# A transformer block on one core: squares of branch and output weights moved to other units, some merge and norm steps reordered, one tail chunk's weights asked for later

## The chip, the cores and the metric

The kernel runs on one core of a Trainium2 chip. The metric is device time in microseconds (us) of one execution. A core has a matrix engine (PE in the profile, with its weight load PEld), three elementwise engines (VectorE, DVE; ScalarE, ACT; GpSimd, POOL) and SyncE (SP), whose queue issues nearly all DMAs here. Each engine works through its own instructions in the order in which the program lists them, and waits at an instruction whose inputs or buffers are not ready. So what a step costs depends on its place in its engine's list.

## What is computed

One layer on 2048 tokens of width 1024, in float32:

```
h    = rms_norm(x) * gain
proj = h @ w_in          # q,k,v of branch A; q,k,v of branch B in 3 groups; gates ga, gb; merge logits mg
ya   = banded attention A (8 query heads, 2 key heads, window 128, sink logit), per-head norm of q and k
yb   = three dilated attentions (dilation 1, 4, 16; 8 heads each), combined by softmax denominators
br_a = (ya * silu(ga)) @ w_branch_a ;  br_b = (yb * silu(gb)) @ w_branch_b
g    = sigmoid(mg + b_merge)
out  = x + (g[0]*br_a + g[1]*br_b) @ w_out
```

## The kernel before

**Number format.** Every float32 operand of a matmul is split into two float16 parts, high and low, and a product is three float16 matmuls (high-high, low-high, high-low). Weights are first scaled by a power of two. For that scale the sum of squares of the weights is needed: ACT squares a piece with a running sum per partition (`w_square`, `g_square`, `piece_square`), a small PE matmul against ones adds the partitions (`norm_sum`, line 219), and six small DVE steps make the power of two (`norm_pow`, line 222 on). For the branch weights a and b and the output weights, one scale each comes from eight *pieces* (`piece_load` line 1160, `piece_square` 1165, two halves of 128x1024 each; `piece_sum` and `piece_pow` at the end). A piece is only squared: the weights themselves are loaded again in the tail.

**Stages.** A start (about 70 us) norms and transposes x into XH and XL. Then come 14 *units* of 8 *pairs* each, 112 pairs: unit 0 and 2 are branch A (4 query heads, one key head), the others branch B (2 heads of one dilation group). A pair projects two blocks of 128 tokens (48 matmuls of 128x384, line 735), norms and splits q and k, transposes them by DMA (`kq`), and computes attention items of earlier pairs: logits (line 905), `maxima` (line 920, with the bias added), exps, a split, a transpose by DMA (`pt`), and the product with the values (line 954). Some pairs also carry a *fill*: 24 matmuls of 128x512 for a gate chunk (line 359). Units 4, 7, 10 and 13 are dilation group 0, in which the three groups are merged for each quarter (`b_merge_q`): `collect` (POOL, line 1118), `exponents` (DVE), exps (ACT), `factors` (DVE), `products` (POOL), `sums` (DVE); since an item runs nearly five pairs behind its projection, half of a unit's merges fall into the next unit, 5, 8 or 11 (or behind the last pair). A merged half goes to a `YPart`: `halves` (ACT, line 1034), `turn_halves` (a DMA transpose on SP, line 1038, `ya<-yh`), `join` (ACT, line 1043), `gate` and `top` (DVE), `store`. The tail (from about 1366 us) makes the merge gates, the branch products and the output product in a form with seven instead of eight block products, for which sums of blocks of x are made during the units (`x_sums`).

**The order of the work.** It is written out by hand. Every step is given a time in units of one pair (in the tail, in us); a heap sorts the steps by time, and they are put into the program between the matmuls in this order. The times do no more than set the order on each engine and each DMA queue. `NORM` holds the times, from the end of a pair, of: square, stats, newton, scale, gain, hi, lo, swap, turn (steps of q and k). `B_MERGE` holds collect, exponents, exps, factors, products, sums; `A_MERGE` those of branch A, whose fourth value is the time of the first product. `Y_DMA` holds load, halves, turn_halves, join, gate, top, store. A B item's steps stand at `LAGS['B']` from a time of 0.387 or 0.887 in a pair, its `out` at 0.223 or 0.723 two pairs on, and its `z_store` (a DMA issued by ACT, line 993) 0.1 behind.

**Raw weights.** One tile of 128x8x384 (`wraw`, one buffer) takes in turn the next unit's weights (`w_load`, from 0.4 in a unit) and, from 5.9 on, a *window*: the gate chunk in its first third, if the unit prepares one (units 2, 4, 7, 10, 13 and two early ones), and a piece in the other two thirds. `N_PREP` holds, in a unit, the time of the first of four piece loads of 256 KB (`B_GAP[2]` = 0.231 apart) and of the two piece squares. In the tail `T_P` holds for each chunk n the times of its weights' preparation (`prep`: load at +0.3, gains from +5.5, squares from +8.5, sum at +15.6, power at +16.1, split from +17.0) and of its T blocks (`w_sums`).

```
    for k in range(8):
        u = 3 + k
        ...
        for j in range(4):
            at(t + N_PREP[0] + B_GAP[2] * j, piece_load, u, k, j)
        for half in range(2):
            at(t + N_PREP[1 + half], piece_square, u, k, half)
    chain([(98.0, piece_sum), (98.3, piece_pow)])
```

Of the kernel before, what the change touches and what calls it, by code (L numbers as in the profile page):

```python
# [63 lines left out]
NPAIR = 8 * NU  # L64

EVAC = (0.015, 0.025, 0.099)
NORM = (0.028, 0.136, 0.32, 0.626, 0.744, 0.904, 0.962, 1.033, 1.118)
LS = 2.887
LAGS = {'A': (-0.21, 0.002, 0.019, 0.144, 0.276, 0.337, 0.417), 'B': (-0.156, -0.001, 0.042, 0.169, 0.19, 0.379, 0.525)}
LV = {'A': 1.111, 'B': 1.829}  # L70
OUT = 0.007
B_LAST = 0.763
DRAIN = 0.8
A_MERGE = (0.085, 0.258, 0.51, 0.671, 1.503, 0.761)
B_MERGE = (-0.037, 0.133, 0.333, 0.507, 0.665, 1.053)
Y_PART = (-0.097, 0.483, 0.709, 0.893, 0.943)
Y_DMA = (-0.097, 0.45, 0.55, 1.05, 1.13, 1.2, 1.25)
Y_MAX_DMA = (0.026, 1.4, 1.45)
GATE = (-0.123, -0.064, 0.329)
W_STEP = (0.4, 0.465, 1.9, 0.445, 4.197, 0.146, 0.342)  # L80
W_MAX = (3.762, 3.892)
G_PREP = (5.907, 6.882, 7.102, 7.671, 7.712, 7.812, 7.942)
N_PREP = (6.3, 7.15, 7.753)
B_GAP = (0.4, 0.138, 0.231)
Y_FREE = 0.15
G_LATE = {6: 0.2, 9: 0.2, 7: 0.2}
Y_MAX = (0.026, 0.815, 0.839)
Y_MAX_A = (0.026, 1.9, 1.95)
X_LOAD = (15.23, 15.24, 18.98, 18.99, 23.61, 30.1, 23.62, 30.09, 30.58, 30.56, 30.55, 30.57, 33.96, 32.57, 32.55, 34.01)
X_SQ = (18.89, 18.9, 18.99, 19, 24.3, 30.11, 24.51, 30.24, 30.89, 30.62, 30.62, 30.62, 37.13, 44.55, 39.37, 40.39)  # L90
X_GROUPS = {(0,): (19.24, 19.72, False), (1,): (19.75, 19.76, False), (2, 3): (19.9, 20.54, False), (4, 5, 6, 7): (30.37, 30.48, False), (8, 9, 10, 11): (30.9, 33.71, False), (12, 13, 14, 15): (44.56, 44.57, False)}
# [9 lines left out]
X_END = (68.1, 71.1, 75.1)  # L101
X_TH = 1.2
X_SC = (0.25, 0.25, 0.25, 0.0625)
X_SUM = ((3, 14.5), (19, 33), (48, 60.5), (71.5, 84.5), (97, 108)), 0.35, 109.0
T_Y = (2.0, 0.8, 1.6, 1.5, 4.0, 26.0, 0.5, 1.3, 2.1, 1.6, 2.0)
T_P = ((0, 0.0, 0.03), (1, 7.0, 31.0), (2, 37.5, 60.5), (3, 69.4, 92.4), (4, 105.8, 128.8), (5, 142.2, 165.2))
T_O = ((2, 38.0, 48.0), (3, 68.0, 80.0), (0, 104.0, 116.0), (1, 140.0, 152.0))
T_OB = ((2, 40.0), (3, 50.0))
T_G = (173.0, 183.0, 193.0, 194.5)
# [21 lines left out]
def block_kernel(tc, x, w_units, w_gate, w_mrg, w_brn, w_out, w_bra, gain, qkg, sink, bias_a, bias_b, b_merge, out):  # L131
# [329 lines left out]
    def chain(steps):  # L461

        steps = sorted(steps, key=lambda e: e[0])
        done = [0]

        def go(k):
            if done[0] < k or steps[k][1](*steps[k][2:]) is False:
                at(now[0] + .04, go, k)
            else:
                done[0] = k + 1  # L470

        for k, e in enumerate(steps):
            at(e[0], go, k)
# [245 lines left out]
    class Pair:  # L719
# [19 lines left out]
        def plan(self, e):  # L739
# [4 lines left out]
            steps = (self.square, self.stats, self.newton, self.scale, self.gain, self.hi, self.lo, self.swap, self.turn)  # L744
            for d, f in zip(NORM, steps):
                at(e[1] + d, f)
# [327 lines left out]
    def a_merge(t, un, za, q):  # L1074
# [21 lines left out]
        def product(c):  # L1096
            y = wk.tile([128, 4, 2, HD], F32, name="ya")
            hs = slice(2 * c, 2 * c + 2)
            G.tensor_tensor(y[:], za[:, :, hs, 0:HD], e1[:, :, hs].unsqueeze(3).to_broadcast([128, 4, 2, HD]), OP.mult)
            YPart(2 * j + c, q, y[:].rearrange("p b h e -> p b (h e)")).plan(t + A_MERGE[3 + c] + A_MERGE[5])  # L1100

        for d, f in zip(A_MERGE, (exponents, exps, factors)):
            at(t + d, f)
        for c in range(2):
            at(t + A_MERGE[3 + c], product, c)

    def b_merge_q(t, un, zz, q):
# [31 lines left out]
        def sums():  # L1139
# [5 lines left out]
            if q % 2:  # L1145
                YPart(4 + j, q // 2, un.y).plan(t + B_MERGE[5] * (B_LAST if t > NPAIR + 1 else 1))

        for d, f in zip(B_MERGE, (collect, exponents, exps, factors, products, sums)):
            at(t + d * (B_LAST if t > NPAIR + 1 else 1), f)
# [58 lines left out]
        chain([(t + G_PREP[1] + .1 * i, g_gain, c, i) for i in range(2)]  # L1208
              + [(t + d, f, c) for d, f in zip(G_PREP[2:6] + (G_PREP[6] + G_LATE.get(c, 0),), (g_square, g_sum, g_pow, g_hi, g_lo))])
    for k in range(8):  # L1210
        u = 3 + k
        t = 8 * u
        if all(w != u for _, w, _ in FILLS):
            at(t + G_PREP[0] - .01, window, u)
        for j in range(4):
            at(t + N_PREP[0] + B_GAP[2] * j, piece_load, u, k, j)
        for half in range(2):
            at(t + N_PREP[1 + half], piece_square, u, k, half)
    chain([(98.0, piece_sum), (98.3, piece_pow)])
    for q in range(4):  # L1220
        fill.setdefault(NPAIR + q, []).extend((mg_step, q, k) for k in range(2))

# [42 lines left out]

    at(X_SUM[2], xs_early)
    times = spread(128, X_SUM[0])
    for k in range(8):
# [4 lines left out]
    while t < NPAIR or heap or any(k >= t for k in fill):  # L1273
        u, j = divmod(t, 8)
# [645 lines left out]
```

## Time and profile before

| | |
|---|---|
| time, median of 3 executions | 1900.66 us (1900.16 to 1904.5) |
| profiled execution | 1902.51 us, of which 1900.7 us span of the core |
| start | 0 to 70 us |
| 14 units | 70 to 1295 us |
| last items, merges and fills | 1295 to 1366 us |
| tail | 1366 to 1901 us |
| B pair without a fill, unit 5 | 9.3 us |
| A pair, unit 2 | 12.5 us without a fill, 17.8 with one |

The profile is of one execution. An engine is *busy* while it works on an instruction, not while it waits. For PE the ends are modelled, and a new matmul starts while the one before is still in the pipeline; therefore a stand of PE shorter than that overlap does not show as idle. The list of waits says for each engine and line what ended the idle time before it, with the total, the number of times and the longest. The table by stage gives the busy time of each engine in a stretch of the span; the stretch less PE's busy time is PE's idle time there. A timeline gives, for one engine, start, length, line, operation, out<-in and, in brackets, the idle time before it and what ended it; `SPq` and `ACTq` are DMA issues of these engines. The granted clock is 1.00 throughout.

### The profile page before, as it was taken

What the parts mean: (1) busy time and instruction counts of PE and PEld (TensorE: products, weight loads), DVE (VectorE), ACT (ScalarE), POOL (GpSimd) and SP (SyncE); (2) the same over time, 40 slices, a digit from 0 to 9 for tenths busy, and PEclk for the clock granted to TensorE, in tenths of its full rate; (3) what the DMA queues carried; (4) which work ended last, traced back from release to release, by engine and by line L of the source; (5) the groups of instructions that cost most, each with busy time, mean ns of one, the idle gap of its engine ahead of it and who ended that gap; (6) DMA issues with size and microseconds to landing.
All of it is one profiled execution on the core that took longest, in us unless ns stands there. A gap on an engine that the chain in (4) does not pass through costs nothing.

```text
span 1900.7 us, 39497 instructions
## 1 busy us (share of the span) xinstructions
PE 1882.0 (99%) x13493; PEld 1182.4 (62%) x13493; DVE 1379.7 (73%) x3691; ACT 1157.6 (61%) x2692; POOL 762.6 (40%) x1782
## 2 busy tenths in 40 slices
PE   8999999999999999999999999999999999999999
PEld 6556666677766687666876668865444444444444
DVE  7579886898887777878778787878457565767412
ACT  8468776787776776777767776666345553422100
POOL 2233343334455554555555654455110001222543
PEclk9999999999999999999999999999999999999999
DMA  8559988798978787798877978678455445988763
GB/s 290 126 98 181 219 166 164 151 184 182 203 145 185 151 174 162 151 183 152 176 153 145 196 139 167 123 180 184 149 196 172 143 146 189 294 252 256 252 245 145
DMA packets 643929, 340.68 MB, mean 179 GB/s; under 512 B 493840, under 2 KB 577424, under 8 KB 642320
## 3 DMA queue, kind: packets, MB, share of 16 engines
q1 hardware_dynamic: 625296, 329.51, 73.2%
q10 hardware_dynamic: 18432, 8.66, 1.9%
q8 instruction: 105, 1.72, 0.4%
q14 instruction: 96, 0.79, 0.1%
HBM read 141.97 MB, written 77.33 MB: 115 GB/s over the span
## 4 chain that ended last, share of the span: by engine, by line
PE 74%; DVE 9%; DMA 6%; ACT 4%; issue 3%; POOL 3%; SPq 1%; DVEq 0%; ACTq 0%; POOLq 0%
PE pj L735 38%; PE pj L359 11%; PE fps L359 6%; PE s L905 5%; PE fps L1787 5%; PE pv L954 4%; PE fps L1575 2%; PE pj L1787 2%; DMA wraw<-in_w_mrg_dram 1%; PE pj L1575 1%; DMA kq<-spl 1%; PE pj L635 1%; DVE wl L279 1%; DMA mtd<-mm 1%; DVE pr L920 1%
## 5 line engine op out<-in xcount | busy, mean ns | idle before, releaser
L735 PE MATMUL pj<-wh,XH 128*128 128x384 f16 x1792 | 584.6, 326 | 4.0 <-DVE vt L767 3.3
L735 PE MATMUL pj<-wh,XL 128*128 128x384 f16 x1792 | 586.2, 327 | 0.0
L735 PE MATMUL pj<-wl,XH 128*128 128x384 f16 x1792 | 584.8, 326 | 0.0
L735 PEld LDWEIGHTS <-XH 128*128 128x128 f16 x3584 | 411.2, 116 | 154.3 <-issue 5.7
L735 PEld LDWEIGHTS <-XL 128*128 128x128 f16 x1792 | 207.6, 116 | 67.4
L920 DVE CUSTOM_DVE_ANT_0 pr<-s,b,ubuf 128x256 f32<-128x256 f32 (+3 forms) x512 | 218.4, 463 | 36.9 <-PE s L905 36.0
L937 DVE SCALAR_TENSOR_TENSOR p<-pr,p 128x512 f16<-128x512 f32 (+2 forms) x256 | 190.4, 744 | 17.8 <-ACT p L933 16.1
L812 POOL COPY spl<-spl 128x256 f16<-128x256 f16 (+1 forms) x224 | 89.5, 428 | 229.7 <-DVE spl L807 227.3
L933 ACT ACTIVATE p<-pr 128x512 f16<-128x512 f32 (+2 forms) x256 | 159.0, 621 | 6.1 <-DMA pt<-p 0.2
L905 PE MATMUL s<-kq 128*128 128x256 f16 (+3 forms) x1168 | 147.9, 254 | 2.0 <-DMA kq<-spl 1.8
L752 ACT ACTIVATE rw<-pj 128x256 f32<-128x256 f32 (+1 forms) x224 | 86.1, 385 | 103.4 <-PE pj L735 95.2
L954 PEld LDWEIGHTS <-pt 128*128 128x128 f16 x3024 | 125.4, 97 | 35.3 <-DMA pt<-p 1.5
L797 POOL TENSOR_TENSOR rw<-rw,g 128x256 f32<-128x256 f32 (+1 forms) x112 | 92.4, 825 | 122.9 <-DVE rw L791 82.3
L954 PE MATMUL pv<-vt,pt 128*128 128x65 f16 (+1 forms) x3024 | 132.7, 193 | 1.1 <-DMA pt<-p 1.1
L905 PEld LDWEIGHTS <-kq 128*128 128x128 f16 x1184 | 101.5, 98 | 43.6 <-DMA kq<-spl 3.5
L310 POOL TENSOR_TENSOR rs_t<-rs_y 128x8 f32<-128x8 f32 (+1 forms) x112 | 44.4, 396 | 208.9 <-DVE rs_y L302 174.3
L791 DVE TENSOR_TENSOR rw<-rw,qr 128x512 f32<-128x512 f32 (+1 forms) x112 | 86.8, 775 | 54.0 <-POOL qr L319 53.6
L1728 POOL TENSOR_TENSOR kp<-kp,fg 128x512 f32<-128x512 f32 x32 | 45.4, 1421 | 190.6 <-DVE fg L1721 190.6
L1787 PEld LDWEIGHTS <-M 128*128 128x128 f16 x684 | 66.9, 98 | 78.8 <-issue 0.6
L359 PE MATMUL fps<-Y,wh 128*128 128x512 f16 x384 | 114.2, 379 | 0.0
L928 ACT ACTIVATE pr<-pr,z 128x128 f32<-128x128 f32 (+2 forms) x256 | 98.7, 438 | 24.3 <-DVE z L920 24.1
L1787 PE MATMUL fps<-wt,M 128*128 128x512 f16 (+1 forms) x516 | 110.3, 374 | 0.3 <-DVE pr L1802 0.3
(289 smaller groups left out, 3838.4 us busy)
## 6 DMA issues: line engine op xcount, KB each, us to landing
wraw<-in_w_units_dram SPq DMA_DIRECT2D x56, 384.0 KB, 4.5
mtd<-mm SPq DMA_DIRECT2D x56, 256.0 KB, 3.9
M<-mtd SPq DMA_DIRECT2D x8, 1792.0 KB, 9.7
zd<-z ACTq DMA_DIRECT2D x128, 66.0 KB, 2.6
zz<-zd SPq DMA_DIRECT2D x64, 132.0 KB, 2.8
xt<-in_x_dram SPq DMA_DIRECT2D x16, 512.0 KB, 9.4
gtd<-yo SPq DMA_DIRECT2D x32, 256.0 KB, 3.0
xsd<-sx SPq DMA_DIRECT2D x32, 256.0 KB, 3.1
```

Source lines behind the costliest of these rows:

```text
L359: out.append(lambda w=w, xx=xx, ch=ch, i=i: T.matmul(ps[:], lhsT=w[:, ch, c0:c0 + 128], rhs=xx[:, ch, ts], start=(i == 0), stop=(i == n - 1)))
L735: out.append(lambda lhs=lhs, rhs=rhs, ch=ch, k=k: T.matmul(ps[:, :384], lhsT=lhs[:, ch, :], rhs=rhs[:, ch, :], start=(k == 0), stop=(k == ...
L791: V.tensor_tensor(q, q, self.rr[:, :n].unsqueeze(2).to_broadcast([128, n, HD]), OP.mult)
L797: G.tensor_tensor(k, k, GT[un.br][:].unsqueeze(1).unsqueeze(1).to_broadcast([128, 2, un.nk, HD]), OP.mult)
L812: G.tensor_copy(sp[:, i, nh:, :, :], sp[:, i, nq:nh, ::-1, :])
L905: T.matmul(self.sv[j][:, o:o + k1 - k0], lhsT=q[:, h, qo:qo + 128], rhs=kt[:, un.nq + kh + v * un.nk, k0:k1], start=(v == 0), stop=(v == 1))
L920: V.tensor_tensor_reduce(out=self.pv[:, j, self.p0:self.p0 + W], in0=self.sv[j], in1=un.bias[:, self.h0 + j, self.b0:self.b0 + W], scale=I ...
L928: A.activation(v, v, AF.Exp, bias=self.stat(j), scale=-1.0)
L933: A.activation(self.sp[:, :128 * n], self.pr, AF.Copy, scale=PSC)
L937: V.scalar_tensor_tensor(self.sp[:, 128 * n:], self.pr, PSC, self.sp[:, :128 * n], OP.mult, OP.subtract)
L954: T.matmul(self.po[:, j, :w], lhsT=p[:, n * j + s, :], rhs=un.v[key][:, vh, c0:c0 + w], start=(k == 0 and s == 0), stop=(k == 2 and s == n ...
L1787: mm.append(lambda ch=ch, k=k, w=w, i=i: T.matmul(ps[:, :cols.stop - cols.start], lhsT=m[:, a, ch, k, :], rhs=wt[w][:, b, ch, cols], start ...
```

## The change

Nothing is added to or taken from the computation, and no tile changes. Times are changed, so steps change places:

- The eight pieces are loaded and squared in units 2, 3, 4, 6, 7, 9, 10 and 12 (`PIECE_U`) instead of 3 to 10; units 5 and 8 have none. Their loads start at 6.473 instead of 6.3 in the unit; the squares keep their times, 7.15 and 7.753. `piece_sum` moves from 98 to 107.
- In `NORM`, stats moves from 0.136 to 0.172 and hi from 0.904 to 0.841.
- In `B_MERGE`, collect moves from -0.037 to 0.034 and exponents from 0.133 to 0.278; in `A_MERGE`, the first product from 0.671 to 0.753.
- In `Y_DMA`, turn_halves moves from 0.55 to 0.576 and join from 1.05 to 1.042; two times of `Y_MAX_A` move by 0.003 and 0.018.
- In `X_SUM`, the fourth stretch for the sums of x starts at 71.842 instead of 71.5, which spreads all 128 steps a little differently, and the early loads of the sums for the tail go from 109 to 111.19.
- In `T_P`, the preparation of tail chunk 1 starts at 10.0 instead of 7.0 us.

```diff
-NORM = (0.028, 0.136, 0.32, 0.626, 0.744, 0.904, 0.962, 1.033, 1.118)
+NORM = (0.028, 0.172, 0.32, 0.626, 0.744, 0.841, 0.962, 1.033, 1.118)
...
-A_MERGE = (0.085, 0.258, 0.51, 0.671, 1.503, 0.761)
-B_MERGE = (-0.037, 0.133, 0.333, 0.507, 0.665, 1.053)
+A_MERGE = (0.085, 0.258, 0.51, 0.753, 1.503, 0.761)
+B_MERGE = (0.034, 0.278, 0.333, 0.507, 0.665, 1.053)
 Y_PART = (-0.097, 0.483, 0.709, 0.893, 0.943)
-Y_DMA = (-0.097, 0.45, 0.55, 1.05, 1.13, 1.2, 1.25)
+Y_DMA = (-0.097, 0.45, 0.576, 1.042, 1.13, 1.2, 1.25)
...
-N_PREP = (6.3, 7.15, 7.753)
+N_PREP = (6.473, 7.15, 7.753)
 B_GAP = (0.4, 0.138, 0.231)
+PIECE_U = (2, 3, 4, 6, 7, 9, 10, 12)
+PIECE_SUM = 107.0
...
-Y_MAX_A = (0.026, 1.9, 1.95)
+Y_MAX_A = (0.023, 1.882, 1.95)
...
-X_SUM = ((3, 14.5), (19, 33), (48, 60.5), (71.5, 84.5), (97, 108)), 0.35, 109.0
+X_SUM = (((3, 14.5), (19, 33), (48, 60.5), (71.842, 84.5), (97, 108)), 0.35, 111.19)
...
-T_P = ((0, 0.0, 0.03), (1, 7.0, 31.0), (2, 37.5, 60.5), (3, 69.4, 92.4), (4, 105.8, 128.8), (5, 142.2, 165.2))
+T_P = ((0, 0.0, 0.03), (1, 10.0, 31.0), (2, 37.5, 60.5), (3, 69.4, 92.4), (4, 105.8, 128.8), (5, 142.2, 165.2))
...
     for k in range(8):
-        u = 3 + k
+        u = PIECE_U[k]
         t = 8 * u
...
-    chain([(98.0, piece_sum), (98.3, piece_pow)])
+    chain([(PIECE_SUM, piece_sum), (PIECE_SUM + 0.3, piece_pow)])
```

## The prediction, made before the changed kernel ran

> **What bounds the kernel now.** I read the page's busy table first, then who TensorE (PE) waits for, then the busy time by stage, and last the engines in order of time around the few stages where PE stands still.
>
> ```profile
> span 1900.7 us, 39497 instructions
> ...
> PE 1882.0 (99%) x13493; PEld 1182.4 (62%) x13493; DVE 1379.7 (73%) x3691; ACT 1157.6 (61%) x2692; POOL 762.6 (40%) x1782
> ```
>
> PE is busy for 1882.0 of 1900.7 us. The change removes no matmul. So nothing in it can bring more than the 18.7 us in which PE stands still, and a step that is taken off another engine is worth only what ends a PE wait sooner. The waits of PE say what ends them (in all, times, longest):
>
> ```profile
> PE pj L735 <- DVE vt L767: 3.3, 5, 0.8
> PE fps L219 <- ACT wl L247: 2.2, 2, 1.8
> PE s L905 <- DMA kq<-spl: 1.8, 1, 1.8
> PE pv L954 <- DMA pt<-p: 1.1, 1, 1.1
> ```
>
> The table by stage tells where. Columns: length, then busy time of PE, weight load, VectorE (DVE), ScalarE (ACT), GpSimd (POOL), then granted clock, DMA share and GB/s.
>
> ```profile
> 0.00:75.00 75.00, 68.68 (x439) 44.12 (x440) 56.52 (x161) 57.02 (x111) 18.97 (x20) 1.00 0.74 228
> 75.00:490.00 415.00, 413.04 (x3655) 282.58 (x3654) 344.82 (x905) 304.28 (x693) 154.88 (x417) 1.00 0.83 167
> 656.50:668.20 11.70, 9.63 (x82) 6.79 (x81) 7.27 (x22) 8.70 (x20) 4.33 (x14) 1.00 1.22 201
> 812.60:899.70 87.10, 86.25 (x667) 57.80 (x666) 67.83 (x211) 61.44 (x148) 50.51 (x123) 1.00 0.85 167
> 899.70:928.00 28.30, 28.17 (x243) 23.29 (x242) 21.31 (x69) 19.59 (x49) 12.69 (x41) 1.00 0.93 189
> 1053.70:1140.50 86.80, 86.20 (x667) 57.72 (x666) 69.52 (x215) 60.37 (x147) 50.67 (x123) 1.00 0.83 162
> 1140.50:1150.80 10.30, 9.51 (x82) 6.93 (x81) 5.82 (x20) 6.43 (x15) 3.30 (x13) 1.00 0.68 142
> 1150.80:1366.00 215.20, 214.83 (x1655) 146.18 (x1654) 162.62 (x504) 130.79 (x343) 104.15 (x271) 1.00 0.70 155
> 1366.00:1395.00 29.00, 27.19 (x128) 12.25 (x127) 10.71 (x22) 12.01 (x22) 4.03 (x4) 1.00 0.93 299
> ```
>
> The start, which the change leaves alone, holds 6.32 us of the idle time. Units 0 to 3 (75 to 490) hold 1.96; the last pair of unit 5 (656.5 to 668.2) 2.07; the last pair of unit 11 (1140.5 to 1150.8) 0.79; units 8 and 11 before their last pairs 0.85 and 0.60; unit 8's last pair with the two behind it 0.13; everything from unit 12 to the tail 0.37; the first 29 us of the tail 1.81. These nine stretches, less the start, make 8.58 us: that is about all the change can win.
>
> **The pieces leave units 5 and 8.** Units 5, 8 and 11 follow the units that merge branch B, carry the second half of that merge, and have the same fills. Only unit 11 has no pieces. So it is the model of what 5 and 8 become. In all three ACT stands at `join` (L1043) for the transposed `ya`, the key split `hi` (L803) is behind it, and PE soon runs out:
>
> ```profile
> 657.13 1.36 ACT L1043 ACTIVATE yh<-ya 128x1024 uint16<-128x1024 uint16 x1 [2.34 <-DMA ya<-yh]
> ...
> 1138.84 0.33 ACTq L993 DMA_DIRECT2D zd<-z  x1
> 1141.64 1.37 ACT L1043 ACTIVATE yh<-ya 128x1024 uint16<-128x1024 uint16 x1 [2.83 <-DMA ya<-yh]
> 1142.87 0.60 ACT L803 ACTIVATE spl<-rw 128x512 f16<-128x512 f32 x1
> ```
>
> ACT waits as long without pieces (2.83 us in unit 11) as with them (2.34 in unit 5), so the pieces do not cause that wait. What they add in unit 5 is behind it: the key transposes then go out among the piece loads at a DMA share of 1.22, against 0.68 in unit 11. So unit 5 should go from 2.07 to unit 11's 0.79: -1.28. Unit 8 pays nothing today at that place with its pieces; between 0 and +0.79 I take +0.2. The pair behind unit 8 can give back at most 0.13: -0.1.
>
> **`join` and `hi` in ScalarE's order.** In a B pair (1.0 of planner time) one item stands at 0.887, so its `z_store` (line 993) is planned at 0.823 and `join` at 0.826. With 1.042, `join` moves to 0.818, ahead of `z_store`; `hi` moves from 0.904 to 0.841 and stays behind both. So where ACT stands at `join`, the 0.33 us of `z_store`'s issue, which today passes before that wait (1138.84), now falls between it and `hi`, and evacuation and PSUM release (L752, L761, L767) come 0.33 later. Units 5, 8 and 11 each have one such place: +0.33 in 5 and 11, and in 8 it is inside the +0.2. The zd written there is read two units later; nobody waits.
>
> In the pair after a unit's first, `hi` at 0.841 now goes ahead of the first two weight squares (0.9):
>
> ```profile
> L244 ACT ACTIVATE wl<-wraw,gn x112: 598/605/624, 47.5 to 1183.7; 128x384 f16<-128x384 f32 x112
> ```
>
> So keys are ready up to 1.2 us sooner once per unit and the squares 0.6 later. PE waits in none of these places, so I take 0; the squares are needed by `w_sum` 1.9 pairs on.
>
> **The merge steps.** `collect` (0.686 to 0.757) goes behind `gain` on POOL; `exponents` (0.856 to 1.001) goes behind `maxima` and the key's `lo` on DVE.
>
> ```profile
> 1054.75 0.19 POOL L1118 COPY zz<-nmB 128x4 f32<-128x4 f32 x1
> ...
> 1057.15 0.18 DVE L1122 TENSOR_TENSOR bm_e<-bm_n,zz 128x12 f32<-128x12 f32 x1
> 1057.25 0.47 DVE L920 CUSTOM_DVE_ANT_0 pr<-s,b,ubuf 128x256 f32<-128x256 f32 x1
> ...
> 1058.66 0.28 DVE L767 SCALAR_TENSOR_TENSOR vt<-pj,vt 128x128 f16<-128x128 f32 x1
> ```
>
> `maxima` thus starts about 0.3 us earlier (two small instructions) and `gain` 0.2 earlier. But both stay ahead of `v_lo` (L767), which is what PE waits for in the first pairs of units 8 and 11: the same work stands before it, so the 0.85 and 0.60 us stay. The merge's exps at 1.056 on ACT, queued behind the item's exps, now waits for `exponents` up to some tenths, with the item's `hi` behind it; `maxima`'s 0.3 pays that back. Sum 0. `stats` at 0.172 goes behind the gate weights' `lo` in units 5, 8 and 11 and behind one `maxima` in A units; a delay of about 1.3 us (1059.91 below) which the scale step 0.45 pair later covers.
>
> ```profile
> 1059.91 1.28 DVE L412 SCALAR_TENSOR_TENSOR gl<-wraw,ubuf,gh 128x1024 f16<-128x1024 f32 x1
> ```
>
> **The pieces come to units 2 and 12.** Unit 12 has room: 0.37 us of PE idle in the 215 us around it. Unit 2 is an A unit whose window also loads gate weights, and it is full:
>
> ```profile
> 366.80:379.30 12.50, 12.50 (x144) 8.57 (x141) 11.46 (x31) 10.63 (x23) 3.86 (x11) 1.00 1.02 207
> 379.30:391.90 12.60, 12.60 (x155) 9.09 (x152) 12.18 (x33) 11.12 (x23) 7.15 (x14) 1.00 0.94 168
> 391.90:409.80 17.90, 17.90 (x171) 13.22 (x168) 17.16 (x47) 15.95 (x34) 6.38 (x19) 1.00 0.91 164
> ```
>
> The next fence has the length of a B pair (its first figure), the squares, their only wait, and the landing of half of the piece loads:
>
> ```profile
> 647.20:656.50 9.30, 9.30 (x82) 6.88 (x81) 6.87 (x20) 6.25 (x15) 3.77 (x13) 1.00 0.93 189
> ...
> L1167 ACT ACTIVATE wraw<-wraw x16: 1039/1046/1069, 493.9 to 1052.9; 128x1024 f32<-128x1024 f32 x16
> L1167 ACT ACTIVATION_READ_ACCUMULATOR wraw<-wraw x16: 180/187/198, 494.8 to 1053.9; 128x1 f32 x16
> ...
>   DMA wraw<-in_w_out_dram: 0.9, 1
> ...
> DMA to landing us min/median/max: 2.9/4.1/6.3
> ```
>
> Two squares of 1.05 + 0.19 make 2.5 us on top of ACT's 11.12 in a 12.6 us pair: 13.6, so ACT falls 1 us behind and makes it up in the next pair (15.95 of 17.9). The projections alternate between two PSUM banks, so an evacuation has half a pair in hand, and the cost lies between 0 and 2.5; I take +0.4.
>
> **Piece loads later everywhere.** Loads start at 6.473 instead of 6.3, so all four pass behind the next item's `pt` transpose (0.412) or the later one (0.912) on SP's queue. The first square still comes at 7.15, so its second load has 0.446 instead of 0.619 pair: in a pair of 9.3 us (the row above) 4.1 instead of 5.8 us. Against the landing row (2.9/4.1/6.3) ACT now waits 0 at the median and 2.2 at worst, in each of eight units. Behind it stand an `out` and the evacuation, which waits for PE anyway:
>
> ```profile
> ACT rw L752 <- PE pj L735: 95.2, 92, 3.3
> ```
>
> 95.2 us over the 92 evacuations that wait is 1.0 us of cover each, and I take 0. By the Trainium skill ("DMA: Bandwidth & Descriptors", Anatomy of one DMA, given for GpSimd's path) a transfer costs about 2.0 us plus bytes over 436 GB/s; for 256 KB I estimate 2.6 us, by which no square would ever wait and the slower case below would drop out. The median of 4.1 here, beside other transfers, speaks against relying on that.
>
> **The tail chunk.** `T_P` moves chunk 1's load, gains, squares, sum and power all 3.0 us later.
>
> ```profile
> 1376.50 4.60 SPq L195 DMA_DIRECT2D wraw<-in_w_mrg_dram  x4
> 1381.20 1.82 SPq L1581 DMA_DIRECT2D mgd<-fd  x2
> ...
> 1389.83 0.63 ACT L247 ACTIVATE wl<-wraw 128x512 f16<-128x512 f32 x1 [0.28 <-POOL wraw L200]
> ...
> 1390.60 0.17 PE fps L219
> ```
>
> Today PE comes to the sum matmul (L219), waits 1.8 us for the last square, and goes on at 1390.60, so it came at 1388.8. Three us later in PE's order is 1391.8. The load was held until 1376.5 by the queue ahead, not by its plan (7.3 us after 1366), so at 10.3 it starts almost as before, only behind one `fd` store: 0.91 us. The squares end near 1391.5, before PE comes: -1.8. Were the load really 3 us later, the gain would be 0. The chunk's T blocks are due at 31.0 as before; they end about a microsecond later, some 2 us ahead of their matmuls.
>
> **The rest.** The T-sums of x move by at most 0.34 pair, A merges by 0.08; both act where PE idles 1.96 us in all (75 to 490), so a gain is at most that, a loss of that size is possible, taken 0. `piece_sum` (three powers, some 18 small DVE steps) moves to unit 13's third pair with as much room as today's; `xs_early`'s tiles are read only in the tail, over four pairs later. Both 0.
>
> **Sum.** -1.28 + 0.33 (unit 5) + 0.2 (unit 8) - 0.1 (behind it) + 0.33 (unit 11) + 0.4 (unit 2) - 1.8 (tail) = -1.9 us. The profiled execution took 1902.51 (span 1900.7 and 1.8 around it), 1.85 above the median of 1900.66. So 1900.6 for such an execution and **1898.8** as the median. About 0.3%, 5.7 us, is what a measurement tells from no change.
>
> **The rivals.** (1) *More waits go than I count.* Keys split ahead of the squares, transposes ahead of piece loads, `maxima` ahead of `exponents` and shifted x sums also end the 8.58 us. All of it: 1892.1; three quarters: 1894.2. For it: nearly all these waits end in a transpose or in DVE's order. Against: none of the moved steps passes `v_lo`. (2) *The tail gain does not arrive* since the load slips the full 3 us behind SP's stores, and unit 5 keeps its wait: without the 1.8 and the 1.28 the sum is +1.2, 1901.8. The load's 1376.5 start speaks against it. (3) *Slower: ACT waits for piece loads.* At the worst landing the first square waits 2.2 us in eight units; past the 1.0 us of cover 1.2 x 8 = 9.6 goes to PE: 1908.4. It decides once loads land over about 5.1 us (4.1 + 1.0) after issue, on busy queues such as units 2, 3 and 4. For it: loads go out behind transposes, DMA share near 1. Against: a square waited only once, 0.9 us, in the trace of before, and pieces fit today in units as full.
>
> **How the numbers follow.** Forecast 0.56 (its own range 1896.5 to 1901.5), rival 1 0.18, rival 2 0.12, rival 3 0.14. Faster by over 0.3% is rival 1: 0.18; slower is rival 3: 0.14; the others are within: 0.68. The range 1893.0 to 1904.5 takes in most of rival 1 and all of rival 2, with the runs' spread (1900.16 to 1904.5); outside stay rival 3 and the end of rival 1, 0.2.
>
> **What would show it.** Right: no PE wait at L219 near 1390, PE idle under 1.2 us at the end of unit 5, about 1.1 at the end of unit 11, `join` directly followed by `zd<-z`, units 2 and 12 with PE idle under 0.5. Wrong: L1167 among ACT's long waits for DMA, a new PE wait in units 2 and 3, or idle gone from 75 to 490 and from the first pairs of 8 and 11.

## The result, and the profile after

The changed kernel takes 1912.08 us (median of four executions, 1910.44 to 1914.06) against 1900.88 for the kernel before in the same session (1900.16 to 1904.5): a ratio of 1.0056, 95% interval 1.0038 to 1.0073. That is slower by 11.2 us, outside the predicted range, on the side of rival 3 and 3.7 us beyond its price. In the kernels from here on every line number is 2 higher than before (L735 is now L737, `hi` L805, the piece loads L1165, their squares L1169).

The profile's page and its list of waits (in all, times, longest), changed kernel:

```profile
span 1911.6 us, 39478 instructions
...
PE 1885.1 (99%) x13493; PEld 1182.6 (62%) x13493; DVE 1384.0 (72%) x3691; ACT 1154.6 (60%) x2692; POOL 769.6 (40%) x1782
```

```profile
PE pj L737 <- DVE vt L769: 6.3, 8, 1.3
PE fps L221 <- ACT wl L249: 2.6, 1, 2.6
PE s L907 <- DMA kq<-spl: 2.1, 2, 1.4
PE pt L221 <- DVE wm L228: 1.5, 1, 1.5
```

The span grew by 10.9 us, PE's busy time by 3.1, so 7.8 us are new idle time; of the 3.1 us, 1.7 are PE at a lower clock in the tail, shown below, and the others stay open. The waits of before at L735 (3.3) have nearly doubled; the one at the tail's sums of squares is still there, at 2.6 instead of 2.2, but at another chunk; the one for L228 (DVE's first step of a power of two) is new. The table by stage of the changed kernel (length, then busy time of PE, weight load, DVE, ACT, POOL, then clock, DMA share, GB/s), cut at the starts of pairs:

```profile
379.30:393.90 14.60, 12.90 (x153) 8.88 (x150) 13.36 (x38) 12.20 (x27) 6.26 (x13) 1.00 1.04 229
660.20:669.50 9.30, 9.30 (x82) 6.88 (x81) 6.70 (x21) 5.61 (x15) 3.42 (x14) 1.00 0.82 149
741.90:815.40 73.50, 72.48 (x592) 46.77 (x591) 58.00 (x178) 53.46 (x150) 40.05 (x113) 1.00 0.81 157
984.70:1058.20 73.50, 72.36 (x592) 46.80 (x591) 56.76 (x176) 53.80 (x150) 40.10 (x113) 1.00 0.80 160
1145.50:1154.80 9.30, 9.30 (x82) 6.87 (x81) 6.93 (x22) 5.55 (x15) 3.76 (x14) 1.00 0.72 150
1253.10:1263.80 10.70, 9.22 (x73) 5.77 (x72) 8.72 (x36) 5.89 (x18) 5.95 (x17) 1.00 0.63 109
```

These are the last pair of unit 2 (12.6 before), the last of unit 5 (11.7 before), unit 7, unit 10, the last pair of unit 11 (10.3 before) and a pair of unit 13 (9.0 before). Units 7 and 10 had no idle time before:

```profile
740.60:812.60 72.00, 72.00 (x592) 46.88 (x591) 58.58 (x178) 53.79 (x149) 38.84 (x113) 1.00 0.82 163
...
981.70:1053.70 72.00, 72.00 (x592) 46.87 (x591) 57.93 (x177) 54.61 (x151) 38.96 (x113) 1.00 0.83 164
```

So the two ends of units that the prediction argued about got better than it said, and time went where it saw little or nothing: +2.0 at the end of unit 2, +1.5 each in units 7 and 10, +1.7 in unit 13, +1.0 in unit 3 and +5.2 from 1286 us on (the start of the last pair).

ACT's waits ahead of the piece squares, by tensor (total, times), changed kernel; before it was one wait of 0.9:

```profile
  DMA wraw<-in_w_out_dram: 8.7, 5
  DMA wraw<-in_w_bra_dram: 7.4, 5
```

16.1 us at ten of the 16 squares. The loads themselves are no slower than before on the median; this is their landing:

```profile
DMA to landing us min/median/max: 3.0/3.9/6.8
```

Before it was 2.9/4.1/6.3. What moved is their place. The end of unit 9 in order of time, POOL's `swap`, SP's queue and ACT:

```profile
978.11 0.74 POOL L814 COPY spl<-spl 128x256 f16<-128x256 f16 x2 [1.49 <-DVE spl L809]
...
979.36 3.95 SPq L822 DMA_TRANSPOSE kq<-spl  x2
...
982.94 0.27 ACT L988 ACTIVATE z<-pv 128x130 f32<-128x130 f32 x1
...
983.36 0.57 SPq L1165 DMA_DIRECT2D wraw<-in_w_out_dram  x1
...
986.52 1.06 ACT L1169 ACTIVATE wraw<-wraw 128x1024 f32<-128x1024 f32 x1 [3.31 <-DMA wraw<-in_w_out_dram]
...
987.57 0.61 ACT L805 ACTIVATE spl<-rw 128x512 f16<-128x512 f32 x1
988.09 0.36 ACT L754 ACTIVATE rw<-pj 128x256 f32<-128x256 f32 x1
```

The fourth load of the piece (planned 7.166 in the unit, 6.993 before) now stands behind the key transposes `turn` (7.118). They occupy SP for 3.95 us, the load goes out at 983.36, lands 3.1 us later, and ACT stands still for 3.31 us at the second square, with `hi` and the evacuation behind it. In these rows the transposes wait for nothing, as their input was ready at 978.85; SP's time goes into issuing them. For all transposes of the keys, the issue takes (min/median/max, ns):

```profile
L822 SPq DMA_TRANSPOSE kq<-spl x224: 1209/1233/2917, 87.4 to 1321.7; - x112
```

So two of them cost SP about 2.5 us at least. At the end of unit 7 a wait comes on top: SP is done with the third load at 808.82 and stands until the first half of `swap` ends:

```profile
808.25 0.57 SPq L1165 DMA_DIRECT2D wraw<-in_w_out_dram  x1
810.90 2.54 SPq L822 DMA_TRANSPOSE kq<-spl  x2
813.50 0.57 SPq L1165 DMA_DIRECT2D wraw<-in_w_out_dram  x1
```

The Trainium skill ("DMA: Bandwidth & Descriptors", Anatomy of one DMA) says that the wait for a DMA's inputs is spent on the sequencer that issues it; these last rows agree, with 2.1 us.

### The profile page after: what moved, and what is told of

It is laid out like the page before. It is cut to its first block, busy times and chain, and to the rows that moved or that the text cites. A ratio compares the mean times of both kernels' runs of the same rounds, so it can differ in the third digit from the quotient of the medians.

```text
span 1911.6 us, 39478 instructions
## 1 busy us (share of the span) xinstructions
PE 1885.1 (99%) x13493; PEld 1182.6 (62%) x13493; DVE 1384.0 (72%) x3691; ACT 1154.6 (60%) x2692; POOL 769.6 (40%) x1782
## 4 chain that ended last, share of the span: by engine, by line
PE 60%; DVE 13%; DMA 7%; POOL 7%; issue 6%; ACT 5%; SPq 1%; ACTq 0%; DVEq 0%; POOLq 0%
PE pj L737 26%; PE pj L361 10%; PE fps L1577 6%; PE fps L1789 4%; PE s L907 4%; PE pv L956 3%; PE fps L361 3%; PE pj L1577 2%; PE pj L1789 2%; DMA kq<-spl 1%; DVE qss L781 1%; DMA mtd<-mm 1%; DVE p L939 1%; DVE spl L809 1%; DVE pr L922 1%
## 5 line engine op out<-in xcount | busy, mean ns | idle before, releaser
L737 PE MATMUL pj<-wh,XH 128*128 128x384 f16 x1792 | 584.3, 326 | 7.0 <-DVE vt L769 6.3
L737 PE MATMUL pj<-wh,XL 128*128 128x384 f16 x1792 | 586.0, 327 | 0.0
L737 PE MATMUL pj<-wl,XH 128*128 128x384 f16 x1792 | 584.6, 326 | 0.0
L737 PEld LDWEIGHTS <-XH 128*128 128x128 f16 x3584 | 411.0, 116 | 158.2 <-issue 10.1
L737 PEld LDWEIGHTS <-XL 128*128 128x128 f16 x1792 | 207.6, 116 | 67.5
L939 DVE SCALAR_TENSOR_TENSOR p<-pr,p 128x512 f16<-128x512 f32 (+2 forms) x256 | 186.9, 730 | 14.7 <-ACT p L935 14.2
L799 POOL TENSOR_TENSOR rw<-rw,g 128x256 f32<-128x256 f32 (+1 forms) x112 | 93.7, 836 | 109.3 <-DVE rw L793 72.5
L754 ACT ACTIVATE rw<-pj 128x256 f32<-128x256 f32 (+1 forms) x224 | 85.5, 382 | 78.7 <-PE pj L737 66.4
L805 ACT ACTIVATE spl<-rw 128x512 f16<-128x512 f32 (+1 forms) x112 | 71.7, 640 | 92.7 <-POOL rw L799 88.5
```

The source lines that it names most:

```text
L737: out.append(lambda lhs=lhs, rhs=rhs, ch=ch, k=k: T.matmul(ps[:, :384], lhsT=lhs[:, ch, :], rhs=rhs[:, ch, :], start=(k == 0), stop=(k == ...
L799: G.tensor_tensor(k, k, GT[un.br][:].unsqueeze(1).unsqueeze(1).to_broadcast([128, 2, un.nk, HD]), OP.mult)
L939: V.scalar_tensor_tensor(self.sp[:, 128 * n:], self.pr, PSC, self.sp[:, :128 * n], OP.mult, OP.subtract)
```

## The experiments

Each kernel was timed in five rounds beside the kernel before, which took 1901.45 to 1902.53 us there. The theory after the result: the loads behind `turn` make ACT wait, and that is the loss. The rival: ACT's waits are hidden, and something else in the change is the loss. It came out between the two. What follows reads one table, of lengths in us (from the first of a pair's projection matmuls to the first of the next stretch, one profiled execution each; "loads ahead" and "norm back" are the changed kernel with that one thing taken back, the three "late" columns the kernel before with late loads alone, with `stats` and with `hi` moved too; the last row is ACT's waiting ahead of the piece squares):

| stretch | before | after | loads ahead | late alone | late + stats | late + hi | norm back |
|---|---|---|---|---|---|---|---|
| last pair of unit 2 | 12.6 | 14.6 | 13.1 | 12.6 | 12.7 | 12.6 | 14.7 |
| unit 3 | 106.2 | 107.2 | 107.2 | 106.6 | 108.1 | 106.5 | 106.0 |
| last pair of unit 5 | 11.7 | 9.3 | 9.3 | 9.6 | 10.5 | 10.5 | 9.3 |
| unit 7 | 72.0 | 73.5 | 72.0 | 72.0 | 72.0 | 74.6 | 72.0 |
| unit 10 | 72.0 | 73.5 | 72.0 | 72.0 | 72.0 | 72.2 | 73.2 |
| last pair of unit 11 | 10.3 | 9.3 | 9.3 | 9.8 | 9.3 | 10.0 | 10.2 |
| fourth pair of unit 13 | 9.0 | 10.7 | 9.0 | 9.0 | 9.0 | 9.0 | 10.2 |
| ACT waits at squares | 0.9 | 16.1 | 2.5 | 16.3 | 14.8 | 18.1 | 13.3 |

**The loads.** From the changed kernel, the loads put ahead of the key transposes, or all the way back:

```diff
-N_PREP = (6.473, 7.15, 7.753)
+N_PREP = (6.42, 7.15, 7.753)    # loads_ahead_of_turn
+N_PREP = (6.3, 7.15, 7.753)     # loads_back
```

> The changed kernel (1912.1 us), with the first piece load at 6.42 instead of 6.473, so that only the fourth load of each piece goes ahead of the key transposes on SP's queue again (and a few loads ahead of a pt transpose). Loads theory: the fourth load, queued behind the key transposes that wait for their data, is what makes ScalarE stand 16.1 us at ten piece squares, and that costs PE about 2.5 us in the first pairs of units 4, 7, 8, 10 and 11: ScalarE's waits at the squares fall under 4 us, the time to about 1909.5. Rival, the merge order (exponents behind maxima and lo) makes those PE waits: ScalarE's waits fall, but the time stays at 1912 within 1.

1905.03 us, ratio 1.0015 (1.0006 to 1.0024): some 7 us of the loss go, with a shift of the loads by 0.053 of a pair. Units 7, 10 and 13 are at their old lengths.

> The changed kernel with the piece loads back at 6.3, ahead of the pt transpose as well. Loads theory: about 1909 us, ScalarE's waits at squares near 1 us as in the kernel before, and the 2 us that PE lost at the end of unit 2 stay, since they come from the piece being there at all. If the place behind the pt transpose were what counts, this one gains and the one at 6.42 does not. Rival (merge order): 1912 within 1.

1907.25 us, 1.0025 (1.0014 to 1.0035). ACT waits 1.0 us at the squares; the last pair of unit 2 still takes 15.2 us. So a good half of the loss hangs on the late loads. The reverse, late loads in the kernel before:

```diff
-            at(t + N_PREP[0] + B_GAP[2] * j, piece_load, u, k, j)
+            at(t + N_PREP[0] + B_GAP[2] * j + (0.14 if j == 3 else 0), piece_load, u, k, j)    # fourth_behind_turn
-N_PREP = (6.3, 7.15, 7.753)
+N_PREP = (6.473, 7.15, 7.753)                                                                # loads_late_alone
```

> The kernel before (1902.5 us in these runs), with one edit: the fourth load of each piece 0.14 of a pair later, so that on SP it stands behind the two key transposes; squares, units and all else as before. Loads theory: ScalarE waits at the second square of nearly every piece, 10 us or more in all against 0.9, and PE loses 3 to 6 us in the pairs behind: 1905.5 to 1908.5. Rival: the fourth load alone costs under 1 us, since ScalarE's wait is covered by its idle time, and the loss needs the merge steps' new order as well: 1903.

1900.82 us, 0.9995 (0.9985 to 1.0006). ACT waits 13.0 us at eight second squares, and no time is lost: the rival holds.

> The kernel before with all four loads of a piece 0.173 of a pair-unit later (6.473 in place of 6.3) and nothing else of the change. Theory of the loads alone: the later first three loads, passed by the pt transposes, add 0.6 to 1.3 us of waiting at the first squares to the 13 us that the fourth load alone gave at the second, and that is what uses up ACT's idle time: the time rises by 5 to 8 us (ratio 1.003 to 1.004) and ACT waits some 16 us at the squares. Rival, a partner in the change: ACT waits as much, 13 to 18 us, and TensorE loses no more than 1 us (ratio within 0.001 of 1).

1901.84 us, 0.9997 (0.9988 to 1.0006), with as much waiting at the squares, 16.3 us, as in the changed kernel. So the late loads alone cost nothing. They cost only together with something else.

**The partner.** Late loads in the kernel before, with the norm steps moved together and one by one:

```diff
-NORM = (0.028, 0.136, 0.32, 0.626, 0.744, 0.904, 0.962, 1.033, 1.118)
+NORM = (0.028, 0.172, 0.32, 0.626, 0.744, 0.841, 0.962, 1.033, 1.118)    # loads_late_norm
+NORM = (0.028, 0.172, 0.32, 0.626, 0.744, 0.904, 0.962, 1.033, 1.118)    # late_stats
+NORM = (0.028, 0.136, 0.32, 0.626, 0.744, 0.841, 0.962, 1.033, 1.118)    # late_hi
-N_PREP = (6.3, 7.15, 7.753)
+N_PREP = (6.473, 7.15, 7.753)                                            # in all three
```

> The kernel before with the late loads and the norm steps in their new order, nothing else. If the norm order is the partner (the gain step and the high half stand nearer to the squares, so that a late ACT delays them): 5 to 8 us slower than before, while the late loads alone are not. If it isn't, the same time as the late loads alone, within 1 us.

1906.67 us, 1.0025 (1.0015 to 1.0035): the norm order is a partner. In this trace the norm chain of unit 7 runs late: `stats` starts 0.46 of a pair in, on the mean, against 0.25 with the late loads alone, and stays late for the whole unit. My guess was that the move of `stats` does this.

> The kernel before with the late loads and of the norm steps only stats at 0.172. Theory: stats is the partner. In the units behind a late second square it starts some 0.2 pair later (0.46 of a pair on the mean of unit 7 in place of 0.25), the whole norm chain behind it, and the lateness lasts the unit; so 3 to 6 us slower than before (ratio 1.0015 to 1.003). Rival (the high half's place): no slower than the late loads alone, within 1 us of before.

1903.64 us, 1.0012 (1.0003 to 1.0021); in unit 7 `stats` is at 0.24 and the length at 72.0. As the cause of the late chain the theory fell. What `stats` does cost is in unit 3 (108.1), and there it needs no late load: 107.2 with the loads ahead, and 106.0 with both norm steps back.

> The kernel before with the late loads and of the norm steps only the high half at 0.841. If stats is the partner: the time of before within 1 us, and stats of unit 7 near 0.25 of a pair. If the high half is: 3 to 6 us slower.

1905.80 us, 1.0018 (1.0009 to 1.0027); `stats` of unit 7 at 0.45, unit 7 at 74.6. The rival was right: in unit 7 the high half is the partner. How it works is seen best between the changed kernel and the one with the high half alone put back:

```diff
-NORM = (0.028, 0.172, 0.32, 0.626, 0.744, 0.841, 0.962, 1.033, 1.118)
+NORM = (0.028, 0.172, 0.32, 0.626, 0.744, 0.904, 0.962, 1.033, 1.118)    # hi_back
+NORM = (0.028, 0.136, 0.32, 0.626, 0.744, 0.904, 0.962, 1.033, 1.118)    # norm_back
```

> The changed kernel with the high half back at 0.904, all else changed. If the high half, waiting on gain with the copy sx and the weight squares behind it, is what turns ScalarE's waits into TensorE's: some 3.4 us of the 11.2 go (1.8 parts in a thousand), so 1908 to 1909, stats of units 7 and 10 near 0.25 of a pair instead of 0.40, and ScalarE still waits 13 us or more at the squares. Rival (in the new places the late loads cost by themselves): within 1 us of the changed kernel.

1908.43 us, 1.0033 (1.0021 to 1.0045): 3.6 us of the loss gone and unit 7 at 72.0, though ACT still waits 13.3 us at the squares. Unit 10 keeps 0.7 of its 1.5 us, and the fourth pair of unit 13 all of its 1.7. ACT in the second pair of unit 6, in order of time, changed kernel:

```profile
688.26 0.63 ACT L805 ACTIVATE spl<-rw 128x512 f16<-128x512 f32 x1 [1.88 <-POOL rw L799]
688.80 0.60 ACT L246 ACTIVATE wl<-wraw,gn 128x384 f16<-128x384 f32 x1
...
689.40 0.60 ACT L246 ACTIVATE wl<-wraw,gn 128x384 f16<-128x384 f32 x1
...
690.52 0.36 ACT L754 ACTIVATE rw<-pj 128x256 f32<-128x256 f32 x1
```

and with the high half back:

```profile
684.13 0.62 ACT L246 ACTIVATE wl<-wraw,gn 128x384 f16<-128x384 f32 x1 [0.40 <-ACT z L988]
...
684.75 0.60 ACT L246 ACTIVATE wl<-wraw,gn 128x384 f16<-128x384 f32 x1
...
685.58 0.63 ACT L805 ACTIVATE spl<-rw 128x512 f16<-128x512 f32 x1
...
686.64 0.36 ACT L754 ACTIVATE rw<-pj 128x256 f32<-128x256 f32 x1
```

With `hi` behind the two weight squares, ACT squares while it waits for `gain` (POOL L799). With `hi` ahead of them it stands for 1.88 us, and then the squares hold up the evacuation (L754), which begins 2.3 us after the start of `hi` in place of 1.1 (`hi` starts 9.1 us into the pair in both). So the next item's norm chain starts later. The start of `stats`, mean over a unit, in fractions of a pair:

| | before | after | hi back | loads ahead |
|---|---|---|---|---|
| unit 6 | 0.18 | 0.32 | 0.21 | 0.33 |
| unit 7 | 0.23 | 0.40 | 0.22 | 0.22 |

With the pieces in the new units, the chain of unit 6 is late wherever `hi` is early, with or without late loads, and no time is lost there. (With the pieces in the old units it goes otherwise: 0.30 with the late loads alone, 0.22 with `hi` early and the loads ahead.) Time is lost in unit 7, and in the kernels here only where `hi` is early and the loads are late. At the end of unit 6 a late chain means a late `turn`, therefore a later fourth load, therefore a longer wait at the second square: 2.89 us in the changed kernel, 1.21 with the high half back, none with the loads ahead. That carries the lateness over into the next unit; with the loads ahead unit 7 starts afresh.

ACT's whole wait for `gain` (total, times), the changed kernel, then the kernel before:

```profile
  POOL rw L799: 88.5, 56
```

```profile
  POOL rw L797: 61.9, 50
```

> The changed kernel with both norm steps back (0.136 and 0.904), all else changed, the loads late. By the pairs measured so far 2.5 parts in a thousand less than the changed kernel: 1906.5 to 1908. Rival: as the kernel with the high half alone back, if stats' place costs nothing here.

1903.54 us, 1.0009 (1.0000 to 1.0018), late loads kept, 8.5 us less than the changed kernel and more than expected. ACT still waits at the squares, and less for `gain` (56.1) than before; two views of this kernel:

```profile
  DMA wraw<-in_w_out_dram: 7.3, 5
  DMA wraw<-in_w_bra_dram: 6.0, 5
```

```profile
  POOL rw L799: 56.1, 46
```

So either half undone, the loads (1.0015) or the norm order (1.0009), takes most of the loss away. Why the norm order weighs more here than the 5 us that it weighed without the new places is open. By the medians, putting `stats` back as well takes 4.9 us more away, where the high half alone took 3.6, so the rival fell; but the traces of the two kernels reach the last pair at the same time (1286.2 and 1286.0 us) and differ behind it (621.0 and 617.3 us), and what `stats` does there is not shown. Nor is unit 10 explained by the norm order: it still takes 73.2 us.

**The places of the pieces and of their sum.**

```diff
-PIECE_U = (3, 4, 5, 6, 7, 8, 9, 10)
+PIECE_U = (2, 3, 4, 6, 7, 9, 10, 12)
-PIECE_SUM = 98.0
+PIECE_SUM = 107.0    # places_107: kernel before with this alone
+PIECE_SUM = 108.4    # loads_late_places: with N_PREP 6.473 too
```

> The kernel before with the late loads and the pieces in units 2, 3, 4, 6, 7, 9, 10 and 12 (their sum behind the last of them, at pair-unit 108.4), nothing else. If the places are the partner: 4 to 8 us slower than before, with 2 us at the end of unit 2, while the late loads alone are not. If they aren't, the same time as the late loads alone, within 1 us, or some 1 us less, since five of the eight units then hold no second chunk.

1908.24 us, 1.0035 (1.0023 to 1.0047). The last pair of unit 2 takes 16.5 us, and in unit 13 the sixth pair takes 14.3 instead of 9.5 and the seventh 11.1 instead of 9.4; other units are unhurt. The time is what the theory said, but this does not show that the places are the partner: 6.5 us stand in unit 13, where PE waits 3.5 us for key transposes and then works at half clock, and the changed kernel has 9.4 us in both of these pairs.

> The kernel before with only the pieces in units 2, 3, 4, 6, 7, 9, 10 and 12 and their sum at pair-unit 107.0, the loads where they were. By the stalls of the changed kernel 2.1 us at the end of unit 2 and 1.6 us at the sum, less 1 us of unit 5: 2 to 4 us slower than before (ratio 1.001 to 1.002). Rival: both stalls need the late loads or the norm order too, and the time is that of before within 1 us.

1904.62 us, 1.0008 (0.9999 to 1.0017): not told apart from no change, though the trace has 1.5 us more in the last pair of unit 2 and 1.9 us more two pairs behind the sum. Against that, the end of unit 5 is at 9.3. Whether the sum makes the 1.9 us is not shown: the same pair takes 10.3 and 10.7 us in the kernels "late + stats" and "late + hi", which have their sum at 98.

From the changed kernel, the sum put behind the power of the next unit's weights:

```diff
-PIECE_SUM = 107.0
+PIECE_SUM = 108.4    # sum_behind_wpow
```

> The changed kernel with the pieces' sum and powers at 108.4 and 108.7 instead of 107.0 and 107.3. Theory: at 107.3 the three powers read the one PSUM bank that unit 14's weight sum, planned at 107.76, needs, and PE stands 1.6 us at that sum: the wait goes, time about 1910.4. Rival: the DVE time of the 18 small steps is what PE waits for, wherever they stand in the unit: a wait of like size appears in the pair after, time 1912.

1912.05 us, 1.0052 (1.0038 to 1.0066): the wait at 1260 us is gone (that pair takes 9.0) and comes back in small pieces in the pairs behind it. The place isn't what is worth changing. With the loads ahead that pair takes 9.0 with no move of the sum at all.

**The tail.**

```diff
-T_P = ((0, 0.0, 0.03), (1, 7.0, 31.0), ...
+T_P = ((0, 0.0, 0.03), (1, 10.0, 31.0), ...
```

> The kernel before with chunk 1 of the tail prepared at 10.0 instead of 7.0 us, nothing else. Tail theory: PE's 1.8 us at chunk 1's sum go and come back at chunk 3's sum as 2 to 4.5 us, more when PE's clock falls behind that wait: 0 to 2.5 us slower, 1902.5 to 1905. Rival: chunk 3's wait needs the later start of the tail's loads that the rest of the change brings: 1.9 us faster, 1900.6.

1903.38 us, 1.0004 (0.9996 to 1.0013), not told apart from no change. In the trace the wait near 1388 is gone as predicted, and 2 us come back 60 us later. First the kernel before, then this one, in order of time at the sum of squares of chunk 3:

```profile
1451.80 0.61 ACT L247 ACTIVATE wl<-wraw 128x512 f16<-128x512 f32 x1
...
1452.81 0.17 PE L219 MATMUL fps<-wsq,ones 128*128 128x4 bf16 x1
```

```profile
1448.84 0.38 PE L1577 MATMUL pj<-XH,wl 128*128 128x512 f16 x1
...
1450.64 0.61 ACT L249 ACTIVATE wl<-wraw 128x512 f16<-128x512 f32 x1
...
1451.39 0.16 PE L221 MATMUL fps<-wsq,ones 128*128 128x4 bf16 x1 [2.18 <-ACT wl L249]
...
1452.30 0.63 PE L1577 MATMUL pj<-XH,wh 128*128 128x512 f16 x1
```

Before, the last square ended 0.4 us ahead of PE. Here PE is there at 1449.05, 3.8 us earlier, and the square only 1.2 earlier (1.8 us of both were gained ahead of the tail), so PE waits 2.2 us. Then a second price: matmuls of 0.38 take 0.63 for 3.4 us. In the changed kernel the same place shows it in the granted clock (the third number from the end, 0.58):

```profile
1458.00:1462.00 4.00, 1.39 (x8) 0.60 (x7) 1.83 (x3) 3.26 (x9) 2.42 (x3) 1.00 0.20 78
1462.00:1466.00 4.00, 4.00 (x13) 1.50 (x12) 3.90 (x10) 2.52 (x5) 0.00 (x0) 0.58 0.18 68
```

That is PE busy and yet slow, a part of the loss (1.7 us) that the busy time hid.

> The changed kernel with the preparation of tail chunk 1 back at 7.0 us. Tail theory: asking for chunk 1 three microseconds later moves the whole row of weight loads in the tail later against PE, and the wait comes back at chunk 3's sum, larger (2.8 us, and some 1.7 us at a lower clock behind it): PE waits about 2 us at chunk 1's sum again and not at chunk 3's, time about 1909.5. Rival: chunk 3's wait comes from what is late when the tail begins, and stays: about 1914.

The changed kernel with chunk 1 at 7.0 again: 1911.77 us, 1.0052 (1.0039 to 1.0064). The wait at chunk 3 is gone, 1.2 us are back at chunk 1, and the time stays. In the profiled executions the part from the start of the last pair on is 2.5 us shorter for it, as the theory said, while what lies ahead is 0.9 longer; so the theory holds for the trace of the tail, but its 1909.5 did not come, and what the tail's step costs in the changed kernel's time is not shown.

**The rest, and what is left.** `join_alone` and `bmerge_alone` are the kernel before with `Y_DMA` or `B_MERGE` as changed.

> The kernel before with the two new values of Y_DMA alone: in the pairs where units 5, 8 and 11 end, join goes ahead of the zd store in ScalarE's order, and nothing else changes places. Store theory: with the store not yet sent, the ya transpose lands in about 3.2 us instead of 4.9, ScalarE stands under 1 us at join instead of 2.3 and 2.8, and PE's idle time at the ends of units 5 and 11 (2.07 and 0.79) goes: 2 to 3 us faster, 1900. Rival, the one on record in the prediction: the store's 0.33 us now falls behind the wait and adds 0.33 us twice: 1903.2. Rival 2: in the changed kernel those waits went since other steps moved: no change.

1901.21 us, 0.9995 (0.9986 to 1.0003). ACT waits at `join` nearly as long as before (1.79 and 2.86 us at the ends of units 5 and 11, against 2.34 and 2.83), so it isn't the store that makes it wait. No cost of 0.33 shows either.

> The kernel before with the new B_MERGE alone (collect behind gain, exponents behind maxima and lo). Theory: v_lo keeps its place, so the units keep their time; behind the last pair the merges of unit 13 get 1 to 2 us slower there (the two PE waits near 1307 and 1323 of the changed kernel): 1903.5 to 1904.5. Rival 1: it also makes the extra 0.5 us in the first pairs of units 8 and 11: 1905. Rival 2: no change.

1901.73 us, 1.0000 (0.9991 to 1.0008): no change.

Taking back what cost, from the changed kernel:

```diff
-N_PREP = (6.473, 7.15, 7.753)
+N_PREP = (6.42, 7.15, 7.753)                      # ahead_tail_back and best_left, with chunk 1 at 7.0
-PIECE_U = (2, 3, 4, 6, 7, 9, 10, 12)
+PIECE_U = (3, 4, 5, 6, 7, 8, 9, 10)               # best_left, with PIECE_SUM 98.0
```

> The changed kernel with the loads ahead of the key transposes again (6.42) and the tail's transposes where they were, all else of the change kept. By the sum of the single runs: 1905.0 of the loads alone taken back, less 0.4 to 1.6 that the tail's step cost, so 1903.4 to 1904.6, a ratio of 1.0005 to 1.001: no gain over the kernel before. Rival: what is left of the change (the waits at the ends of units 5 and 11 gone) brings 2 to 3 us once both costs are away: 1898 to 1900, a ratio of 0.998 to 0.999.

1902.86 us, 1.0007 (0.9998 to 1.0016).

> The changed kernel with loads at 6.42, the tail's transposes, the places of the pieces and the place of their sum as before; what is left are the merge, norm and store steps and the sums of x. If the places cost 2 to 4 us as the stalls say, this is 1 to 2 us faster than before (ratio 0.999 to 0.9995); if they cost nothing, it is the 1.0007 of the kernel with loads and tail alone taken back.

1902.21 us, 1.0002 (0.9993 to 1.0011). Here unit 3 is at 107.6 and the last pair of unit 5 at 11.5. The steps left (merge, norm, store, sums of x) bring nothing, and no version here beats the kernel before. It also closes the square of the two causes. In the old units the norm order without late loads costs nothing (this kernel), late loads without the norm order cost nothing, and both together cost 5 us.

## Why the prediction was wrong

**Piece loads later everywhere (taken at 0).** This step failed, in three ways; taking it back alone (loads ahead) takes 7 of the 11.2 us away. It listed what the loads are moved past on SP's queue as the two `pt` transposes and left out `turn` at 7.118, which the fourth load crosses and which holds SP for 2.5 us or more. It watched the first square, where the waits now are 0 to 1.3 us, and not the second, where they are up to 3.3. And it gave each delay a cover of 1.0 us of ACT's idle time without asking who else in the change draws on that cover. The cover was in fact larger than I said: late loads alone hide 16 us of waiting. But the change spends it twice: with late loads in both kernels, the norm order alone makes 5 us of difference.

**`join` and `hi`: "PE waits in none of these places, so I take 0".** The second failed step. It saw that `hi` passes the first two weight squares of a unit and counted that as a gain for the keys. It did not ask whether `hi` can start there: it has to wait for `gain`, and the squares are what ACT did during that wait. ACT's waits for `gain` went from 61.9 to 88.5 us in all, and both norm steps taken back take 8.5 of the 11.2 us away.

Rival 3 (ACT waits for piece loads, 1908.4, chance 0.14) had the sign and the resource. Its point of decision was wrong: only four of the 32 loads landed later than 5.1 us after issue (median 3.9); most were not slower, they were issued later; and the lateness doesn't cost 1.2 us a unit by itself, but with the order behind it.

**The pieces leave units 5 and 8 (-1.28, +0.2).** The last pair of unit 5 went down by 2.4 us, to 9.3 without any idle time, and so it did in every kernel with the new units. Unit 11 as the model was wrong, and so was the base: other executions with the old units show 9.6 to 11.5 there, so part of the 2.07 was chance in one profile (the kernel with the tail's step alone, the same up to 1366 us, has 10.5). In unit 8 the last pair stayed at 9.3.

**+0.33 in units 5 and 11** didn't come. The end of unit 11 gained 1.0 us instead, which goes with `stats` at 0.172: 9.3 with it in every kernel, 9.8 to 10.4 without. There `join` waits only 0.75 us, and the store passes:

```profile
1144.53 1.38 ACT L1045 ACTIVATE yh<-ya 128x1024 uint16<-128x1024 uint16 x1 [0.75 <-DMA ya<-yh]
1144.53 0.33 ACTq L995 DMA_DIRECT2D zd<-z  x1
1145.77 0.60 ACT L805 ACTIVATE spl<-rw 128x512 f16<-128x512 f32 x1
```

`join` is directly followed by `zd<-z`, as forecast. The store is issued while ACT is at work on `join`, so it delays nothing.

**Unit 2 (+0.4)** was mis-sized: 2.0 us in its last pair here, 1.5 with the places alone, though 0.1 with the high half back. The cover of half a pair for an evacuation was right in kind; the exps behind the square were not counted, and PE waited for them and for the transposes that follow (0.7 and 1.0 us), one of which took 5.7 us to land among the piece loads. Why the high half's place decides here is open.

**The merge steps ("the 0.85 and 0.60 us stay").** They did not: the first pairs of units 8 and 11 wait 1.34 and 1.12 us for `v_lo` in the changed kernel, 1.12 and 0.86 with the new `B_MERGE` alone. No time could be seen in that.

**The tail (-1.8)**: the mechanism was right and 1.97 us came. What failed is the question of what is late next: the text checked the T blocks of the same chunk and not chunk 3's sum, which had only 0.4 us of room. The gain went there and to the slow clock behind it, +4.4 in the changed kernel's trace.

**`piece_sum` "as much room as today's"** was wrong with late loads: 1.48 us of PE wait at 1260, none with the loads ahead.

Against the span of before: units 1 and 5 gained 1.4 and 1.9 us, 9 and 11 together 0.8; units 2, 3, 7, 8, 10 and 13 lost 3.3, 1.0, 1.5, 0.5, 1.5 and 1.8, and the part from 1286 us on 5.2. These are single executions: in the kernel with the tail's step alone, the same code up to 1366 us, units differ from the kernel before by up to 1.1 us. Not settled: 1.3 us in unit 2's second pair, 1.8 us while the last items drain (1295 to 1330), and 0.8 us near 1700, where other kernels scatter by 1 to 2 us as well.

## What to carry to other kernels

Check every move against the whole queue it passes, the transposes that wait for their own inputs above all, and price moves that use the same idle time together: an idle engine hid 16 us of waiting until another edit took away the work that had filled it. In an in-order engine, keep a step that waits (here `hi`) behind the ready work, not ahead of it. Where a stall is taken away, look for the next place where the engine that now comes early meets an unmoved deadline.

## What the runs showed of the hardware

After some waits of PE its matmuls run at half speed for 3.4 us, beginning 0.4 to 1.4 us after work resumes. It was so behind waits of 1.96 us (`ahead_tail_back`), 2.04 (`loads_late_places`), 2.18 (`tail_alone`), 2.28 (`loads_ahead_of_turn`), 2.33 (`late_stats`) and 2.61 (the changed kernel). First the stretches around the wait of 2.04 us at the end of unit 2 (granted clock 1.00, then 0.54), then the one behind the wait of 2.33 us:

```profile
387.00:391.60 4.60, 2.56 (x35) 1.75 (x33) 4.39 (x18) 2.49 (x6) 1.46 (x2) 1.00 1.24 187
391.60:394.90 3.30, 3.30 (x13) 1.62 (x12) 2.45 (x7) 3.30 (x7) 0.00 (x0) 0.54 1.10 244
```

```profile
1393.30:1396.70 3.40, 3.40 (x10) 1.18 (x8) 2.36 (x5) 3.14 (x5) 0.00 (x0) 0.50 0.56 191
```

Other waits of the same length had no such follow-up: 2.12 and 2.41 us in `hi_back`, 2.29 and 2.36 in `loads_back`, 1.98 in `best_left`, 1.8 in the kernel before (at 1388 us). Behind the one of 2.41 us:

```profile
1456.50:1460.50 4.00, 4.00 (x20) 1.79 (x20) 3.97 (x8) 2.98 (x5) 0.00 (x0) 1.00 0.18 68
```

So between 1.96 and 2.41 us the length of the wait does not decide it, and what does is not shown here. The Trainium skill ("TensorE: Matmul & The Clock Gate", Part 1) gives half rate after at least one idle window of about 3.4 us; here shorter waits were at times enough. In the kernel with the tail's step alone, the wait of 2.18 us cost 1.7 us more (eight matmuls at 0.43 instead of 0.215 from start to start).
